# One expert's first weights in transfers of 112, 8 and 8 rows: a mixture-of-experts decoder layer on one core

## The chip, the cores and the metric

The kernel runs on one core of one Trainium2 chip. The metric is the device time of one execution in microseconds (us), as the median of three runs; lower is better. The profile comes from one further execution.

## The reference

One decoder layer over 256 tokens with 1024 features, in float32. Sixteen learned meta tokens are put ahead of the sequence and dropped at the end. With `DEPTH = 1` only the pooling mixer is used, never attention:

```
h = layer_norm(alpha * h + pool_mixer(h))     # trailing means over 2, 4, 8, 16 positions, per-group 256 x 256 matmul
h = layer_norm(alpha * h + moe(h))            # top 4 of 32 experts
```

In `moe` a router picks four of 32 experts for each token. Each expert computes `(clamped_swiglu(x @ w1[e] + b1[e]) @ w2[e] + b2[e]) * gate`, with `w1[e]` of 1024 x 2048 and `w2[e]` of 1024 x 1024 float32 values, 8 MB and 4 MB. All 32 experts have tokens, so some 400 MB of weights are read once from HBM.

## The kernel before

A prologue loads the input, mixes and normalizes it, computes the router's choice, and gives every token a slot in each of its experts. An expert has 64 slots in the main pass; a guarded second pass (`overflow`) covers experts with more tokens.

Then a loop, unrolled in Python, goes over the 32 experts, `for e in range(E)` at line 570. In each step:

- `load_w1` (line 345) issues the loads of `w1[e]`: two tiles of `[128, 4, 2048]`, named `w1t`, one for each half of the contraction. The host has laid out the weights so that partition p of a tile is 32 KB without a gap in HBM. A tile of the first 31 experts is one DMA of 128 rows of 32 KB, 4 MB; for the last expert the second tile comes in three pieces.
- `load_w2` (line 355) issues the loads of `w2`, one expert behind, as one tile `w2t` of the same size. The last expert's `w2` comes in five pieces, `w2h`.
- `mlp_in` (line 388, matmuls at L394) multiplies the gathered tokens by `w1`: 64 matmuls for an expert, 32 on each tile.
- `swiglu` adds the bias, transposes and applies the activation (ACT and DVE); `mlp_out` (matmuls at L443) multiplies by `w2`; `combine` (L462) sums the weighted outputs back into the tokens; `prepare` gathers the tokens of the next two experts (L138).

All weight tiles share one pool of four buffers (`W_BUFS = 4`, tag `"w"`). All their DMAs are issued in program order by SP on one queue. A DMA is issued when PE has read the last of the tile that held the buffer four tiles earlier. One load, `b2r` (33 rows of 4 KB), is issued by ACT on another queue. SP issues nothing but DMAs.

Of the kernel before, what the change touches and what calls it, by code (L numbers as in the profile page):

```python
# [17 lines left out]
P = 128  # L18
# [7 lines left out]
E = 32  # L26
# [8 lines left out]
WARM = 4  # L35
REST = 8
LEN = N_META + SEQ
AUX = 5 * KC + E + KC * E


@with_exitstack
def moe_trunk(ctx: ExitStack, tc: tile.TileContext, x, pool_w, aux_in, b1_in, w1, w2, w2_last, b2, out):
    nc = tc.nc
# [15 lines left out]
    def bank_t(i=None):  # L59
        if i is None:  # L60
            i = turns[0] = 1 - turns[0]
        return bank(f"t{i}", 1)
# [4 lines left out]
    def bank_o(i=None):  # L67
        if i is None:
            i = turns[1] = (turns[1] + 1) % 3
        return bank(f"o{i}", 1)  # L70
# [18 lines left out]
    b2r = const.tile([E + 1, D], F32, name="b2r")  # L89
    aux = const.tile([P, AUX], F32, name="aux")  # L90
    b1 = const.tile([P, 2 * KC * E], F32, name="b1")
# [63 lines left out]
    with tc.tile_pool(name="pro", bufs=1) as pro:  # L155

        xT = pro.tile([P, KC, LEN], F32, name="xT")
        zT = xT[:, :, N_META:]  # L160
# [48 lines left out]
        def pool(g):  # L209
# [3 lines left out]
            while 2 * n < wd:  # L213
                s2 = pro.tile([P, 2, LEN], F32, tag=f"s{n % 3}", name="s2")
                nc.vector.tensor_tensor(s2[:, :, 2 * n - 1:], s[:, :, 2 * n - 1:], s[:, :, n - 1:LEN - n], op=ALU.add)
                s, n = s2, 2 * n
            o, lo = uT[:, g], N_META
            if wd == 2:
                nc.vector.tensor_tensor(o, v[:, :, lo - 1:LEN - 1], v[:, :, lo:], op=ALU.subtract)
            else:  # L220
                nc.vector.tensor_tensor(o, s[:, :, lo:], s[:, :, lo - n:LEN - n], op=ALU.add)
                nc.vector.scalar_tensor_tensor(o, v[:, :, lo:], -float(wd), o, op0=ALU.mult, op1=ALU.add)
# [71 lines left out]
        def last_row(row, dst):  # L294
            for i in range(2):
                nc.scalar.copy(dst[:, i * 512:(i + 1) * 512], spread(row, i, bank_y()))
# [45 lines left out]
    acc = work.tile([P, NT, D], F32, name="acc")  # L342


    def load_w1(src, pieces=((0, 4), (0, 4))):
        v = src.rearrange("(i p j) f -> i p j f", p=P, j=4)
        ts = []
        for i, js in enumerate(pieces):
            wt = wpool.tile([P, 4, 2 * D], F32, tag="w", name="w1t")
            for j, j2 in zip(js, js[1:]):  # L350
                nc.sync.dma_start(out=wt[:, j:j2], in_=v[i][:, j:j2])
            ts.append(wt)
        return lambda k: ts[k // 4][:, k % 4, :]

    def load_w2(src, js=(0, KC)):
        v = src.rearrange("(p j) f -> p j f", j=KC)
        wt = wpool.tile([P, KC, D], F32, tag="w", name="w2t")
        for j, j2 in zip(js, js[1:]):
            nc.sync.dma_start(out=wt[:, j:j2], in_=v[:, j:j2])
        return lambda k: wt[:, k, :].rearrange("p (c o s) -> p o c s", c=2, o=2)  # L360
# [14 lines left out]
    def slot_rows(d, gate, to=bank_t):  # L375

        dg = work.tile([P, NT, 2, CAP], F32, tag="dg", name="dg", bufs=1)
        nc.vector.tensor_mul(dg, d, gate.unsqueeze(3).to_broadcast([P, NT, 2, CAP]))
        s = work.tile([P, 2, SEQ], F32, tag="srow", name="srow", bufs=2)
        p = to()  # L380
        for t in range(NT):
            nc.tensor.transpose(p[:, t * P:(t + 1) * P], dg[:, t].rearrange("p i s -> p (i s)"), ident)
        nc.scalar.copy(s[:, 0], p[:, :SEQ])
        nc.scalar.copy(s[:CAP, 1], p[CAP:, :SEQ])
        nc.scalar.copy(s[CAP:, 1], p[:CAP, :SEQ])
        return s

    def mlp_in(xcols, w1k):
        ph = [bank_h() for _ in range(2)]
        for k in range(KC):  # L390
            wk = w1k(k)
            for u in range(2):
                for hf in range(2):
                    last[k // 4] = nc.tensor.matmul(ph[u][hf * CAP:(hf + 1) * CAP], lhsT=xcols(k),  # L394
                                                    rhs=wk[:, u * D + hf * 512:u * D + (hf + 1) * 512],
                                                    start=(k == 0), stop=(k == KC - 1))
        return ph
# [57 lines left out]
    def outputs():  # L455
        return work.tile([P, 2, 512], F32, tag="y", name="y", bufs=2)

    def combine(y, s, first=False):
        for t in range(NT):
            for o in range(2):  # L460
                p = bank_o()
                nc.tensor.matmul(p, lhsT=s[:, o, t * P:(t + 1) * P], rhs=y[:, o, :], start=True, stop=True)  # L462
                a = acc[:, t, :].rearrange("p (c o s) -> p o c s", c=2, o=2)[:, o]
                pv = p.rearrange("p (c s) -> p c s", c=2)
                if first:
                    nc.vector.tensor_copy(a, pv)
                else:
                    nc.vector.tensor_add(a, a, pv)  # L468
# [70 lines left out]
    def prepare(pair, to=bank_t, banks=(bank_o, bank_o)):  # L539
        d = dispatched(place[:, :, 2 * pair:2 * pair + 2])  # L540
        s = slot_rows(d, gates[:, :, 2 * pair:2 * pair + 2], to)
        xg = columns()
        gather(d, xg, banks)
        pairs[pair] = s, outputs(), xg

    def finish(e, to=bank_y):
        pair, i = divmod(e, 2)
        mlp_out(acts[e], w2s[e], pairs[pair][1], i, to)
# [9 lines left out]
    def by_tile(v):  # L558
        return v.rearrange("p (c o s) -> p o c s", c=2, o=2)

    def onto(y, s, cols, i=None, last=False):

        for t in range(NT):
            for o in range(2):
                r, v = (slice(0, P), o) if i is None else (rows_of(o, 0), o ^ i)
                w = nc.tensor.matmul(z[t][o][:, cols], lhsT=s[r, v, t * P:(t + 1) * P], rhs=y[r, o, cols],  # L566
                                     start=False, stop=last, skip_group_check=True)
        return w

    for e in range(E):  # L570
        pair, i = divmod(e, 2)
        w1k = load_w1(w1[e], ((0, 4), (0, 4) if e < E - 1 else (0, 2, 3, 4)))

        for x in range(max(e - 1, 0), e + (e == E - 3)):
            if e <= E - 3:
                w2s[x] = load_w2(w2[x])
        if i == 0:
            xg = pairs[pair][-1]
        ph = mlp_in(lambda k: xg[k // 4][:, k % 4, i * CAP:(i + 1) * CAP], w1k)
        if e == 0:  # L580
            with tc.issue_after(last[1].ins):
                pairs[0] = slot_rows(d0, gates[:, :, 0:2]), outputs(), xg0
        elif e < E - 3 and i and pair:
            s, y, _ = pairs[pair - 1]
            with tc.issue_after(last[0].ins):
                combine(y, s, pair == 1)
        elif e == E - 3:
            s, y, _ = pairs[pair - 1]
            with tc.issue_after(last[0].ins):
                onto(y, s, slice(0, 512))  # L590
        if e == E - 4:
            z += [[bank_o(), bank_o()], [bank_o(), bank_t(1)]]
            for t in range(NT):
                for o in range(2):
                    nc.tensor.matmul(z[t][o], lhsT=ident, rhs=by_tile(acc[:, t])[:, o], start=True, stop=False,
                                     skip_group_check=True)
        if 0 < e < E - 4:
            finish(e - 1)
        acts[e] = swiglu(ph, b1T[:, :, e, :], (bank_t, bank_t) if e < E - 4 else (t0, bank_y))
        if E - 4 <= e < E - 2:  # L600
            finish(e - 1)
        if e == E - 1:

            nc.scalar.activation(root, acts[e][:, 0, 0:1], AF.Sqrt, scale=0.0, bias=eps_out)
        if i and e < E - 3:
            prepare(pair + 1)
        if e == REST:
            with tc.issue_after(last[1].ins):
                add_rest()
        if e == REST + 4:  # L610
            with tc.issue_after(last[1].ins):
                last_row(b1nT, b1_b)
        if e == E - 3:
            prepare(pair + 1, t0, (bank_h, bank_h))
            finish(e, t0)
            s, y, _ = pairs[pair]
            onto(y, s, slice(0, 512))
# [81 lines left out]
```

## Time and profile before

| what | value |
|---|---|
| median of 3 runs | 969.16 us (969.06 to 969.58) |
| the profiled execution, its own time | 969.38 us |
| its span in the profile | 967.5 us |
| PE busy | 888.6 us, 92% |
| bytes moved by DMA | 407.09 MB, mean 421 GB/s |
| DMA transfers of `w1t` | 66, of which 63 of 4096 KB |

The span is the time from the first to the last instruction in the trace; some 1.9 us of the execution's time lie around it. PE is the matmul engine, DVE and ACT the vector and the scalar engine; SP is the engine that issues the DMAs, and its rows in the timelines are those issues. "DMA share" is the mean busy share of the core's 16 DMA engines.

### The profile page before, as it was taken

The page shows a single profiled execution, that of the slowest core. Times are in us where ns is not written, and L with a number is a line of the kernel's source. Part 1 is how long each engine was busy: PE and PEld are TensorE (multiplying, and loading weights), DVE is VectorE, ACT ScalarE, POOL GpSimd, SP SyncE. Part 2 cuts the span into 40 slices and gives each one's busy share as a digit, 9 for nine tenths or more (in the row PEclk, how much of TensorE's full clock was granted, in tenths as well). Part 3 has the DMA queues.
Part 4 walks back from the last instruction along what each step waited for, and adds up shares of the span by engine and source line. Part 5 has one row for each costly group of instructions (what it writes and reads, how often), then busy time and mean ns, then how long its engine had stood idle before and what let it go on. Part 6 is the DMA issues. An engine that isn't in the chain of part 4 may idle for free.

```text
span 967.5 us, 9682 instructions
## 1 busy us (share of the span) xinstructions
PE 888.6 (92%) x4229; PEld 374.3 (39%) x4229; DVE 237.8 (25%) x495; ACT 132.8 (14%) x271; POOL 1.1 (0%) x9
## 2 busy tenths in 40 slices
PE   9999898989899998998988989799898989999995
PEld 7443333424334343443433434343333433334332
DVE  7331122212043131121311223122121311212024
ACT  1320110201002010020201102011010100102011
POOL 0000000000000000000000000000000000000000
PEclk9999999999999999999999999999999999999998
DMA  9999999999999999999999999999999999999992
GB/s 380 429 430 431 434 430 430 433 427 429 431 430 431 429 431 428 433 429 430 433 429 428 430 430 429 433 432 433 431 429 431 428 428 429 433 433 428 429 415 112
DMA packets 16649, 407.09 MB, mean 421 GB/s; under 512 B 1851, under 2 KB 1979, under 8 KB 3420
## 3 DMA queue, kind: packets, MB, share of 16 engines
q1 hardware_dynamic: 16560, 406.30, 98.0%
q8 instruction: 35, 0.57, 0.2%
q10 hardware_dynamic: 44, 0.14, 0.1%
q14 instruction: 10, 0.08, 0.0%
HBM read 405.38 MB, written 1.05 MB: 420 GB/s over the span
## 4 chain that ended last, share of the span: by engine, by line
PE 53%; DMA 44%; DVE 1%; issue 0%; ACT 0%; DVEq 0%; ACTq 0%
DMA w1t<-in_w 39%; PE ps_h L394 25%; PE ps_y L443 11%; PE ps_o L138 5%; PE ps_o L462 5%; DMA w2t<-in_w 3%; DMA w2h<-in_w_last 2%; PE ps_t L406 2%; PE ps_t L180 1%; PE ps_t L443 1%; PE ps_o L566 1%; PE ps_y L103 0%; PE ps_o L489 0%; PE ps_y L451 0%; PE ps_h L227 0%; PE ps_h L138 0%
## 5 line engine op out<-in xcount | busy, mean ns | idle before, releaser
L394 PE MATMUL ps_h<-w1t,xg 128*64 128x512 f32 x2048 | 469.7, 613 | 48.7 <-DMA w1t<-in_w 48.6
L394 PEld LDWEIGHTS ps_h<-w1t,xg 128*64 128x64 f32 x2048 | 157.5, 141 | 345.0 <-issue 336.7
L443 PE MATMUL ps_y<-w2t,act 128*64 128x512 f32 x928 | 205.5, 595 | 9.9 <-DMA w2t<-in_w 9.1
L408 DVE TENSOR_TENSOR a<-ps_t,b 128x512 f32<-128x512 f32 x60 | 41.5, 692 | 403.4 <-PE ps_t L406 400.3
L443 PEld LDWEIGHTS ps_y<-w2t,act 128*64 128x64 f32 x928 | 67.6, 137 | 128.4 <-issue 113.6
L403 ACT COPY hs<-ps_h 128x512 f32<-128x512 f32 x64 | 37.5, 585 | 351.7 <-PE ps_h L394 351.7
L468 DVE TENSOR_TENSOR acc<-acc,ps_o 128x512 f32<-128x512 f32 x48 | 33.0, 687 | 134.8 <-PE ps_o L462 134.8
L138 PE MATMUL ps_o<-disp,h 128*128 128x128 f32 x448 | 59.1, 275 | 0.0
L138 PEld LDWEIGHTS ps_o<-disp,h 128*128 128x128 f32 x448 | 55.4, 192 | 7.0 <-issue 7.0
L434 DVE COPY y<-ps_y 64x512 f32<-64x512 f32 (+1 forms) x30 | 20.4, 679 | 121.5 <-PE ps_y L443 120.6
L462 PE MATMUL ps_o<-y,srow 128*128 128x512 f32 x104 | 48.1, 605 | 0.0
L432 ACT COPY y<-ps_y 64x512 f32<-64x512 f32 (+1 forms) x30 | 17.2, 572 | 208.7 <-DVE y L434 208.7
L143 ACT ACTIVATE xg<-ps_o,aux 128x128 f32<-128x128 f32 x56 | 21.1, 455 | 177.2 <-PE ps_o L138 177.2
L406 PE MATMUL ps_t<-ident,hs 128*128 128x128 f32 x240 | 39.3, 286 | 1.9 <-ACT hs L403 0.5
L406 PEld LDWEIGHTS ps_t<-ident,hs 128*128 128x128 f32 x240 | 25.2, 141 | 32.0 <-ACT hs L403 30.1
L462 PEld LDWEIGHTS ps_o<-y,srow 128*128 128x128 f32 x104 | 18.7, 189 | 29.2 <-issue 29.2
L416 DVE TENSOR_TENSOR a<-a,sig 128x512 f32<-128x512 f32 x32 | 22.1, 692 | 11.2 <-ACT sig L414 11.1
L414 ACT ACTIVATE sig<-a 128x512 f32<-128x512 f32 x32 | 20.1, 630 | 30.5 <-DVE a L412 28.0
L146 DVE TENSOR_SCALAR xg<-ps_o,aux 128x128 f32<-128x128 f32 x60 | 22.8, 404 | 2.8 <-PE ps_o L138 2.7
L418 DVE SCALAR_TENSOR_TENSOR act<-a,a 128x512 f32<-128x512 f32 x32 | 22.0, 687 | 0.6
L415 DVE TENSOR_SCALAR a<-a 128x512 f32<-128x512 f32 x32 | 13.4, 420 | 0.0
L412 DVE TENSOR_SCALAR a<-a 128x512 f32<-128x512 f32 x32 | 13.3, 417 | 0.0
(163 smaller groups left out, 253.0 us busy)
## 6 DMA issues: line engine op xcount, KB each, us to landing
w1t<-in_w SPq DMA_DIRECT2D x63, 4096.0 KB, 30.2
w2t<-in_w SPq DMA_DIRECT2D x30, 4096.0 KB, 29.0
w2t<-in_w SPq DMA_DIRECT2D x4, 1024.0 KB, 26.8
w2h<-in_w_last SPq DMA_DIRECT2D x3, 1024.0 KB, 19.9
w1t<-in_w SPq DMA_DIRECT2D x1, 2048.0 KB, 26.6
w1t<-in_w SPq DMA_DIRECT2D x2, 1024.0 KB, 29.7
xT<-in_x SPq DMA_DIRECT2D x2, 544.0 KB, 5.3
pw<-in_pool_w SPq DMA_DIRECT2D x2, 512.0 KB, 6.4
```

Source lines behind the costliest of these rows:

```text
L138: nc.tensor.matmul(p[:, (k % n) * P:(k % n + 1) * P], lhsT=h[:, t, k * P:(k + 1) * P], rhs=d[:, t].rearrange("p i s -> p (i s)"), start=(t ...
L143: gx = nc.scalar.activation(xg[0][:, k, :], pk, AF.Identity, scale=g0T[:, k:k + 1], bias=b0T[:, k:k + 1])
L146: nc.vector.tensor_scalar(xg[1][:, k - 4, :], pk, g0T[:, k:k + 1], b0T[:, k:k + 1], op0=ALU.mult, op1=ALU.add)
L394: last[k // 4] = nc.tensor.matmul(ph[u][hf * CAP:(hf + 1) * CAP], lhsT=xcols(k), rhs=wk[:, u * D + hf * 512:u * D + (hf + 1) * 512], start ...
L403: nc.scalar.copy(hs, ph[u])
L406: nc.tensor.transpose(pt[:, j * P:(j + 1) * P], hs[:, j * P:(j + 1) * P], ident)
L408: nc.vector.tensor_add(a, pt.rearrange("p (c s) -> p c s", s=CAP), bias[:, :, u].unsqueeze(2).to_broadcast([P, KC, CAP]))
L416: nc.vector.tensor_mul(gate, gate, sig)
L418: nc.vector.scalar_tensor_tensor(act.rearrange("p c s -> p (c s)"), up.rearrange("p c s -> p (c s)"), 1.0, gate.rearrange("p c s -> p (c s ...
L443: nc.tensor.matmul(py[o], lhsT=act[:, 2 * j + hf, :], rhs=wk[:, o], start=(n == 0), stop=(n == KC - 1))
L462: nc.tensor.matmul(p, lhsT=s[:, o, t * P:(t + 1) * P], rhs=y[:, o, :], start=True, stop=True)
L468: nc.vector.tensor_add(a, a, pv)
```

## The change

`load_w1` gets a list of row ranges, and issues one DMA for each range in place of one for all 128 rows. The list has the one range 0 to 128 for all experts but the 17th (`e == 16`); there it is 0 to 112, 112 to 120 and 120 to 128. The 17th expert's `w1` is thus moved by six DMAs, for each of its two tiles 112 rows (3584 KB), eight rows (256 KB) and eight rows (256 KB). Bytes, buffers, order and everything else stay.

```
+APART = ((0, P - 16), (P - 16, P - 8), (P - 8, P))
...
-    def load_w1(src, pieces=((0, 4), (0, 4))):
+    def load_w1(src, pieces=((0, 4), (0, 4)), rows=((0, P),)):
...
             for j, j2 in zip(js, js[1:]):
-                nc.sync.dma_start(out=wt[:, j:j2], in_=v[i][:, j:j2])
+                for r, r2 in rows:
+                    nc.sync.dma_start(out=wt[r:r2, j:j2], in_=v[i][r:r2, j:j2])
...
-        w1k = load_w1(w1[e], ((0, 4), (0, 4) if e < E - 1 else (0, 2, 3, 4)))
+        w1k = load_w1(w1[e], ((0, 4), (0, 4) if e < E - 1 else (0, 2, 3, 4)),
+                      APART if e == E // 2 else ((0, P),))
```

## Rows read from the trace of the kernel before

**Rows 1.** The page: span, busy time by engine, the chain that ended last.

```profile
span 967.5 us, 9682 instructions
...
PE 888.6 (92%) x4229; PEld 374.3 (39%) x4229; DVE 237.8 (25%) x495; ACT 132.8 (14%) x271; POOL 1.1 (0%) x9
...
PE 53%; DMA 44%; DVE 1%; issue 0%; ACT 0%; DVEq 0%; ACTq 0%
```

**Rows 2.** The page's DMA part: all packets, then queue, kind, packets, MB, share.

```profile
DMA packets 16649, 407.09 MB, mean 421 GB/s; under 512 B 1851, under 2 KB 1979, under 8 KB 3420
...
q1 hardware_dynamic: 16560, 406.30, 98.0%
q8 instruction: 35, 0.57, 0.2%
q10 hardware_dynamic: 44, 0.14, 0.1%
```

**Rows 3.** Windows of 100 us in mid-run; last columns PE clock, DMA share, GB/s.

```profile
400.00:500.00 100.00, 91.95 (x438) 38.28 (x433) 21.71 (x43) 12.90 (x28) 0.00 (x0) 0.98 1.00 430
500.00:600.00 100.00, 92.66 (x436) 39.14 (x436) 25.18 (x49) 13.50 (x28) 0.00 (x0) 0.97 1.00 430
```

**Rows 4.** Waits of the engines: who waited for whom, us, times, longest.

```profile
PE ps_h L394 <- DMA w1t<-in_w: 48.6, 26, 3.1
...
PE ps_y L443 <- DMA w2t<-in_w: 9.1, 8, 1.3
```

**Rows 5.** Waits of SP's queue before it issues, in the same columns.

```profile
SPq L359 <- PE ps_h L394: 285.9, 30, 18.6
SPq L351 <- PE ps_y L443: 242.8, 28, 11.9
SPq L351 <- PE ps_h L394: 227.0, 30, 11.3
```

**Rows 6.** The chain of waits from 895 us to the end: start, us, what.

```profile
899.33 26.61 DMA w1t<-in_w
925.96 19.91 DMA w2h<-in_w_last
945.92 1.95 PE ps_h L451 x16
```

**Rows 7.** DMA issues: count, KB of each, median us from issue to landing.

```profile
w1t<-in_w SPq DMA_DIRECT2D x63, 4096.0 KB, 30.2
w2t<-in_w SPq DMA_DIRECT2D x30, 4096.0 KB, 29.0
...
w1t<-in_w SPq DMA_DIRECT2D x1, 2048.0 KB, 26.6
w1t<-in_w SPq DMA_DIRECT2D x2, 1024.0 KB, 29.7
...
aux<-in_aux SPq DMA_DIRECT2D x1, 164.0 KB, 3.1
b2r<-in_b ACTq DMA_DIRECT2D x1, 132.0 KB
```

**Rows 8.** Line 351 from 400 to 600 us: ns of an issue, and landing times.

```profile
L351 SPq DMA_DIRECT2D w1t<-in_w x13: 327/328/328, 401.3 to 578.0; - x13
...
DMA to landing us min/median/max: 26.7/30.3/32.4
```

**Rows 9.** SP's timeline around the 17th expert's two loads: start, us, what.

```profile
448.77 10.08 SPq L351 DMA_DIRECT2D w1t<-in_w  x2
471.41 0.33 SPq L359 DMA_DIRECT2D w2t<-in_w  x1
```

**Rows 10.** PE's timeline at the 17th expert's two halves of L394.

```profile
481.25 7.09 PE L394 MATMUL ps_h<-w1t,xg 128*64 128x512 f32 x32
491.06 8.78 PE L394 MATMUL ps_h<-w1t,xg 128*64 128x512 f32 x32 [2.72 <-DMA w1t<-in_w]
```

## The prediction, made before the change was run

> **What bounds the kernel now.** I read the page from the top, then views by time. First the busy shares and the chain that ended last [rows 1]: PE is busy 92% of the span, which looks like a PE-bound kernel, but the chain is 44% DMA, nearly all of it `w1t`, and the two take turns. Second the DMA part [rows 2]: the main queue's packets fill 98.0% of sixteen engines' time. Third the windows [rows 3]: in mid-run the DMA share is 1.00 and 430 GB/s are moved in both stretches, while PE has 7 to 8 us to spare in each 100. So the sixteen DMA engines never rest, and PE waits for them: the waits [rows 4] put 48.6 us before L394 to `w1t`, in 26 waits of at most 3.1 us. The reader is to see that a microsecond more work for the slowest DMA engine is a microsecond more kernel, while a microsecond of SP's time costs nothing: SP itself waits hundreds of microseconds for PE to free a buffer [rows 5].
>
> The end says the same. The last steps of the chain [rows 6] are 26.61 us of a `w1t` transfer, at once followed by 19.91 us of a `w2h` transfer, and only from 945.92 us on PE and DVE set the pace. What delays the transfers therefore delays the end one for one.
>
> **What a transfer is made of.** The issues [rows 7] show 63 + 1 + 2 of `w1t`; a whole tile is 4096 KB, 128 rows of 32 KB. The main queue's issues, twelve groups on SP from the first row to `aux`, add up to 115, and its 16560 packets [rows 2] are 115 x 144, so each 128-row transfer is 128 row packets and 16 closing ones: sixteen engines, eight rows each. The small queue q10 carried `b2r`, 33 rows of 4 KB, in 44 packets: 33 and 11, so eleven engines with three rows each. Engines are thus counted by what divides the rows. At 430 GB/s an engine moves 26.9 GB/s, and a 32 KB row takes 1.22 us; a tile is 8 x 1.22 = 9.75 us.
>
> **The change, part by part.** Two tile transfers become six. (a) The two of 112 rows: sixteen engines with seven rows each, 8.53 us instead of 9.75, so -1.22 us on every engine and tile. (b) The four of eight rows: eight rows can occupy at most eight engines, one row each. Those eight get two more rows a tile; the other eight get nothing. (c) Four more issues on SP at 0.328 us [rows 8], 1.3 us. They are covered: the two issues for the 17th expert lie at 448.77 us and ten later, and SP next issues at 471.41 [rows 9], after waiting for PE. A transfer lands 26.7 to 32.4 us after its issue, some three transfers deep. Without that cover they would cost 1.3 us. (d) 32 more closing packets (2 x 16 + 4 x 8 against 2 x 16); under (b)'s bounds they vanish. Nothing moves on PE, ACT or DVE.
>
> So the sum hangs on the price of an eight-row transfer to the eight engines that carry it. Lower bound: each engine moves its row at its own speed, 1.22 us. Upper bound: rate goes with the number of partitions written, 8/128 of 430 GB/s, and the 262 KB take 9.75 us, eight times as long. Large transfers that write few neighbouring partitions do not occur in this trace; each big one spreads over all 128, where every engine might well have a way into SBUF to itself. The nearest row is q10, the one load of less than 128 rows. Its 0.1% (0.05 to 0.15%) of 16 x 967.5 = 15,480 us are 7.7 to 23 us for 0.14 MB, 55 to 166 us per MB; q1 has 15,170 us for 406.30 MB, 37.3 us per MB. So 33 rows cost 1.5 to 4.4 times as much per byte. Their packets are short, and that may be a part of it: q8, 16 KB packets, has 23 to 39 us for 0.57 MB, 1.1 to 1.8 times. I take four times, inside the q10 bounds and towards their upper end, because eight neighbouring rows are fewer than 33: 4.87 us for each eight-row transfer.
>
> The sum for those eight engines: 7 + 4 + 4 = 15 row times a tile in place of 8, 7 x 1.22 = 8.5 us, and 17.1 us for two tiles. I count all four on the same eight engines; if they took turns on all sixteen, half of it would be left. Against the profiled execution's own 969.38 us (a span of 967.5 and 1.9 around it) that is 986.5; the median of the runs is 0.2 lower, 986.
>
> [...]
>
> **What is late next.** PE starts the 17th expert's two halves at 481.25 and 491.06, the second after 2.72 us of waiting [rows 10]. It would start them some 8 and 17 us later; nothing gives this back, since DMA is full in every later window [rows 3]. The other eight engines run ahead into the queued transfers and then idle.
>
> **The rivals.**
> *The rows share nothing, and the eight engines were ahead.* Instruction packets (q8, 0.2%) take 23 to 39 us of engine time. If these fall on the eight engines that the short transfers spare, those end the run 2.9 to 4.8 us behind, about 3.9. Taking two rows (2.43 us) from them and giving two to the others moves the last arrival from 3.9 to max(3.9 - 2.43, 2.43) = 2.43 us: 1.5 us gained, 967.7. For it: instruction packets exist and must fall somewhere. Against it: no view names their engines. It ends on the other side, faster by over 0.2% (1.9 us, about what a measurement of this kernel can tell from no change), only when the halves differ by 4.4 us or more: then up to 2.4 us gained, 966.8. I give this rival 0.28: 0.22 within 0.2%, 0.06 faster.
> *The rows share nothing, and the eight engines were not ahead.* Then two rows more are on the slowest engine: +2.43 us, 971.6, slower by 0.25%. For it: DMA busy at 1.00 throughout leaves no engine slack to absorb it. Chance 0.10.
> *The change is hidden.* DMA would need slack later; the windows show none. It is inside the first rival's 0.22.
>
> **How the numbers follow.** The forecast, eight-row transfers well above one row time, has 0.62. Its own range: at twice a row time 7 + 2 + 2 = 11 rows a tile, +7.3 us, 976.5; at the 4.4 of q10's upper bound 15.8 rows, +19 us, 988.2; I put 976 to 990. At eight times it would be +36.6 us, 1006, which I leave out above, with about 0.1. Since the no-change cases hold over 0.2, the whole range reaches down to 967.5, which leaves out only the best of the first rival. Slower 0.62 + 0.10 = 0.72, same 0.22, faster 0.06.
>
> **What the profile of the changed kernel would show.** q1 should have 16560 + 32 = 16592 packets; another number says that the rows were split over other engines. The issue list should show `w1t` x2 of 3584 KB and x4 of 256 KB, and x61 whole. If the forecast holds, mean GB/s falls to about 413 (407.09 MB in 985 us), the waits of L394 for `w1t` rise from 48.6 us by about 17, two of them by some 8 us each between 480 and 520 us, the 256 KB transfers land late, and all from there to the end is shifted by one amount. If the waits near 480 us rise by 2 us or less, the rows share nothing, and a shift at the end of 1 to 2 us in either direction tells the two rivals apart. The prediction is wrong if eight engines write eight neighbouring rows at full speed; then its largest term, 17.1 us, is gone.

## The result

| | before | after |
|---|---|---|
| median of 4 runs | 969.2 us (969.06 to 969.58) | 999.4 us (997.94 to 1000.17) |
| ratio | | 1.0309, 95% interval 1.0291 to 1.0327 |
| the profiled execution, its own time and its span | 969.38, 967.5 | 999.78, 998.0 |

The change costs 30.2 us, 3.1%. The prediction had the direction, but 986 us, and a range that ends at 990. Lines of the body stand three lower than before: L394 is L397, L351 is L354.

The page of the changed kernel, the lines that answer to [rows 1] and [rows 2], with the granted clock and the GB/s in 40 slices:

```profile
span 998.0 us, 9691 instructions
...
PE 888.2 (89%) x4229; PEld 373.5 (37%) x4229; DVE 238.0 (24%) x495; ACT 132.9 (13%) x271; POOL 1.1 (0%) x9
...
PEclk9999999999999999999779999999999999999998
DMA  9999999999999999999999999999999999999992
GB/s 382 434 426 435 427 433 430 430 431 429 430 431 430 432 429 431 429 431 369 198 247 429 433 431 429 430 431 430 431 428 433 429 430 430 429 433 428 427 409 79
DMA packets 16681, 407.09 MB, mean 408 GB/s; under 512 B 1883, under 2 KB 2011, under 8 KB 3452
...
q1 hardware_dynamic: 16592, 406.30, 97.8%
```

PE's work is the same to 0.4 us. Nearly all of the loss lies in three slices near the middle, where GB/s fall from 430 to 198. The DMA line says 9 there as everywhere: the engines were busy, and slow. The packets are the 16592 that were forecast, which fits the counts of engines assumed there. The same stretch in windows of 10 us (in the kernel before these seven windows have 423 to 442 GB/s):

```profile
460.00:470.00 10.00, 10.00 (x53) 5.03 (x53) 2.17 (x4) 1.51 (x4) 0.00 (x0) 1.00 1.08 364
470.00:480.00 10.00, 9.72 (x56) 4.71 (x54) 5.36 (x13) 2.91 (x6) 0.00 (x0) 1.00 0.98 216
480.00:490.00 10.00, 1.30 (x8) 0.14 (x2) 0.68 (x1) 0.58 (x1) 0.00 (x0) 0.71 1.03 175
490.00:500.00 10.00, 3.01 (x8) 1.00 (x10) 0.00 (x0) 0.00 (x0) 0.00 (x0) 0.50 0.98 211
500.00:510.00 10.00, 6.22 (x26) 1.66 (x22) 0.00 (x0) 0.00 (x0) 0.00 (x0) 0.93 1.07 226
510.00:520.00 10.00, 0.00 (x0) 0.00 (x0) 0.00 (x0) 0.00 (x0) 0.00 (x0) 0.58 0.91 210
520.00:530.00 10.00, 8.72 (x32) 2.92 (x32) 0.00 (x0) 0.51 (x1) 0.00 (x0) 0.74 0.98 419
```

The last two columns say it: the DMA share stays near 1, the rate is half. Against 430 GB/s the seven windows lack 66 + 214 + 255 + 219 + 204 + 220 + 11 = 1189 GB/s for 10 us each, which at 430 GB/s is 27.7 us, nearly the whole loss. The half rate already holds from 470 to 480 us, where the first 112-row transfer must run, and not only at the eight-row ones; that is the first sign of which step failed.

The issues, the waits of PE, PE's timeline at the 17th expert's two halves and the next expert's first, and two steps of the chain of waits, in answer to [rows 7], [rows 4], [rows 10] and [rows 6]:

```profile
w1t<-in_w SPq DMA_DIRECT2D x61, 4096.0 KB, 30.1
...
w1t<-in_w SPq DMA_DIRECT2D x2, 3584.0 KB, 50.7
...
w1t<-in_w SPq DMA_DIRECT2D x4, 256.0 KB
```

```profile
PE ps_h L397 <- DMA w1t<-in_w: 79.3, 27, 15.7
```

```profile
496.99 9.23 PE L397 MATMUL ps_h<-w1t,xg 128*64 128x512 f32 x32 [15.69 <-DMA w1t<-in_w]
...
521.27 9.03 PE L397 MATMUL ps_h<-w1t,xg 128*64 128x512 f32 x32 [15.05 <-DMA w1t<-in_w]
...
542.05 8.78 PE L397 MATMUL ps_h<-w1t,xg 128*64 128x512 f32 x32 [3.34 <-DMA w1t<-in_w]
```

```profile
930.14 26.62 DMA w1t<-in_w
956.77 19.87 DMA w2h<-in_w_last
```

The two 3584 KB transfers take 50.7 us from issue to landing in the median, where a whole tile takes 30.1. PE waits 15.69 and 15.05 us for the two halves, and the last two steps of the chain stand 30.8 us later than in [rows 6], with the same lengths: one shift, never given back. From 490 to 500 us the granted clock of PE is 0.50 of full, and the first half's 32 matmuls, begun at 496.99, take 9.23 us in place of the 7.09 of [rows 10]; since PE then waits 15.05 us for the second half anyway, that adds nothing.

### The profile page after: what moved, and what is told of

Its sections match the earlier page's. It is cut to its first block, busy times and chain, and to the rows that moved or that the text cites. A ratio compares the mean times of both kernels' runs of the same rounds, so it can differ in the third digit from the quotient of the medians.

```text
span 998.0 us, 9691 instructions
## 1 busy us (share of the span) xinstructions
PE 888.2 (89%) x4229; PEld 373.5 (37%) x4229; DVE 238.0 (24%) x495; ACT 132.9 (13%) x271; POOL 1.1 (0%) x9
## 3 DMA queue, kind: packets, MB, share of 16 engines
q1 hardware_dynamic: 16592, 406.30, 97.8%
## 4 chain that ended last, share of the span: by engine, by line
PE 53%; DMA 43%; another core or an unknown queue 2%; DVE 1%; ACT 0%; issue 0%; SPq 0%; DVEq 0%; ACTq 0%
DMA w1t<-in_w 36%; PE ps_h L397 25%; PE ps_y L446 11%; DMA w2t<-in_w 5%; PE ps_o L140 4%; PE ps_o L465 4%; DMA w2h<-in_w_last 2%; PE ps_t L409 1%; PE ps_t L182 1%; PE ps_t L446 1%; PE ps_o L569 1%; PE ps_y L105 0%; PE ps_o L492 0%; PE ps_y L454 0%; PE ps_h L229 0%
## 5 line engine op out<-in xcount | busy, mean ns | idle before, releaser
L397 PE MATMUL ps_h<-w1t,xg 128*64 128x512 f32 x2048 | 469.2, 612 | 79.4 <-DMA w1t<-in_w 79.3
L397 PEld LDWEIGHTS ps_h<-w1t,xg 128*64 128x64 f32 x2048 | 157.0, 141 | 376.4 <-issue 350.5
L409 PEld LDWEIGHTS ps_t<-ident,hs 128*128 128x128 f32 x240 | 25.2, 140 | 32.0 <-ACT hs L406 30.1
## 6 DMA issues: line engine op xcount, KB each, us to landing
w1t<-in_w SPq DMA_DIRECT2D x61, 4096.0 KB, 30.1
w1t<-in_w SPq DMA_DIRECT2D x2, 3584.0 KB, 50.7
```

The lines of the kernel that those rows point to most:

```text
L409: nc.tensor.transpose(pt[:, j * P:(j + 1) * P], hs[:, j * P:(j + 1) * P], ident)
```

## The experiments

All edit the loads of the 17th expert's first weights alone, unless said otherwise. Times are medians, "+" is against the kernel before, run beside it on the same chip (969.2 to 969.5 us). The theories, as the expectations name them: A, engines that write partitions which share a way into SBUF (a path that several partitions would have in common; no view shows one) slow each other (in the forecast this was the price of the eight-row transfers alone); B, more and shorter transfers cost something each; C, balance, the two extra rows on eight of the engines; D, the slowness is on the reading side, in HBM.

**More transfers, all rows (e1).** The two tiles are cut by columns into three DMAs each.

```
-        w1k = load_w1(w1[e], ((0, 4), (0, 4) if e < E - 1 else (0, 2, 3, 4)))
+        w1k = load_w1(w1[e], ((0, 2, 3, 4), (0, 2, 3, 4)) if e == E // 2 else
+                      ((0, 4), (0, 4) if e < E - 1 else (0, 2, 3, 4)))
```

> The 17th expert's two tiles are moved in three transfers each, as in the change, but cut by columns: all 128 rows, with 16, 8 and 8 KB of each row. Theory A (shared ways: packets slow one another when engines write partitions that share a way into SBUF, and a 128-row transfer avoids that): no slowing, 969 to 970 us. Theory B (price of more and shorter transfers): about what the change cost, 999 us. Theory C (balance: the cost is the two extra rows on eight engines): 969 us.

969.4 us, ratio 1.0002 (0.9993 to 1.0012). Six transfers in place of two cost 0.2 us, within the interval; B falls.

**Fewer, balanced pieces (e2, e3), and one tile alone (e4).**

```
-APART = ((0, P - 16), (P - 16, P - 8), (P - 8, P))
+APART = ((0, P - 16), (P - 16, P))           # e2
+APART = ((0, P // 2), (P // 2, P))           # e3
-                for r, r2 in rows:
+                for r, r2 in (rows if i == 0 else ((0, P),)):   # e4
```

> 112 and 16 rows for each of the two tiles: every engine has eight rows again, and no transfer has eight. Theory A: the 112-row packets stay at about 2.4 us in place of 1.22, 7 x 1.2 x 2 = +17 us, and the 16 rows cost some 3 us more a tile: 985 to 997 us. Theory B: half as many transfers added, +15, 984 us. Theory C: balanced, 969 us.

> 64 and 64 rows for each of the two tiles, four rows on every engine each time. Theory A: sixteen engines write half of the partitions; if these hold half of the ways, every packet takes twice 1.22 us and a tile 19.5 us in place of 9.75: +19.5 us, 988 to 989 us. Theory B: +15, 984 us. Theory C: balanced, 969 us.

> The change on the first of the 17th expert's two tiles alone. If each tile pays for itself (A, B and C alike): half of 30, 984 us. If the two disturb each other, as a queue that has come apart would: less than half, 975 to 980 us.

e2: 996.0 us, ratio 1.0277 (1.0259 to 1.0294), +26.8. e3: 993.1, 1.0243 (1.0226 to 1.0261), +23.9. e4: 986.9, 1.018 (1.0163 to 1.0197), +17.7. In e2 and e3 every engine has, if rows are counted as in the prediction (7 + 1 and 4 + 4), eight rows a tile, as before, and most of the loss stays: C falls, and with it the picture of the sum, in which only the engines of the short transfers pay. e4 costs a little more than half of the whole.

**Which side of the transfer (e5 to e8).** The first tile alone as sixteen transfers of eight rows: neighbours on both sides (e5), four apart on both sides (e6), four apart in SBUF alone (e7), four apart in HBM alone (e8).

```
+NEAR = [slice(8 * m, 8 * m + 8) for m in range(16)]
+SPREAD = [slice(32 * b + c, 32 * b + c + 29, 4) for b in range(4) for c in range(4)]
+EIGHTS = tuple(zip(NEAR, NEAR))    # SBUF, HBM; e6 SPREAD, SPREAD; e7 SPREAD, NEAR; e8 NEAR, SPREAD
...
-                nc.sync.dma_start(out=wt[:, j:j2], in_=v[i][:, j:j2])
+                for a, b in (rows if i == 0 else WHOLE):
+                    nc.sync.dma_start(out=wt[a, j:j2], in_=v[i][b, j:j2])
```

> The first tile of the 17th expert goes in sixteen transfers of eight neighbouring rows, the second whole. Eight engines have 16 rows in place of eight. Theory C (balance alone): 8 x 1.22 = +9.8 us, 979 us. Theory A: eight neighbouring partitions share two ways, packets of 3.3 us (as seen near 485 us in the changed kernel) to 4.9 us, 16 of them in place of eight at 1.22: +43 to +68 us, 1012 to 1037 us.

> The same sixteen transfers of eight rows, but the eight rows of each are four apart (c, c+4, ... c+28 of a block of 32), in SBUF and in HBM. Same number, size and engines as with neighbouring rows. Theory A, with a way for every four neighbouring partitions: eight ways for eight engines, packets of about 1.22 us, +10 us, 979 us. Theory B and a theory that any eight-row transfer is slow: as with neighbouring rows, 1012 us or more.

> Sixteen transfers of eight rows that are four apart in SBUF but neighbours in HBM; the rows of the tile's weights are thereby in another order, so the 17th expert computes with rows in the wrong place. Theory A (the way into SBUF): about 979 us. Theory D (the reading side: eight neighbouring rows of HBM are slow): as with neighbouring rows, 1012 us or more.

> Sixteen transfers of eight rows that are neighbours in SBUF but four apart in HBM; the 17th expert again computes with rows in the wrong place. Theory A: as with neighbouring rows, 1012 us or more. Theory D: about 979 us.

| | SBUF | HBM | us | ratio | |
|---|---|---|---|---|---|
| e5 | neighbours | neighbours | 999.8 | 1.0326 (1.0305 to 1.0348) | +30.6 |
| e8 | neighbours | four apart | 995.7 | 1.027 (1.0253 to 1.0287) | +26.5 |
| e6 | four apart | four apart | 985.2 | 1.0166 (1.0149 to 1.0183) | +16.0 |
| e7 | four apart | neighbours | 984.9 | 1.0163 (1.0146 to 1.018) | +15.7 |

What decides is which partitions are written together: e7 is e6, and e8 is near e5. D falls as the main cause; that e8 is 4 us below e5, clear of the intervals, is not explained by any run. The window from 470 to 480 us, first of e5, then of e6, and e6's next one:

```profile
470.00:480.00 10.00, 10.00 (x58) 4.74 (x56) 5.37 (x13) 2.91 (x6) 0.00 (x0) 1.00 0.55 139
```

```profile
470.00:480.00 10.00, 10.00 (x58) 4.75 (x56) 5.36 (x13) 2.91 (x6) 0.00 (x0) 1.00 0.50 211
480.00:490.00 10.00, 2.68 (x14) 0.66 (x10) 0.68 (x1) 0.58 (x1) 0.00 (x0) 0.83 0.93 223
```

From 470 to 480 us the DMA share in e6 is 0.50, and 211 GB/s are moved, half of 430: what eight engines would move, each at the rate it has in a whole tile. In e5, with eight neighbours, a little more of the engines' time (0.55) moves 139. The sizes missed: e6 and e7 came out 6 us above their expectation, e5 and e8 below theirs. One thing behind them lies with SP, whose seventeen issues for the 17th expert last until 481.62 us in e6 (the two of [rows 9] end at 458.85):

```profile
448.67 32.95 SPq L356 DMA_DIRECT2D w1t<-in_w  x17
```

Between 440 and 500 us SP waited 26.1 us for `w1t` transfers to land before it issued more. The second tile is the last of the seventeen, so it starts late, and from 470 to 480 us half of the engines' time goes unused (share 0.50). The totals of e5 to e8 hold this cost as well, and are not the price of partitions alone; their comparison, sixteen transfers of one size each, stands.

**The 112-row transfer with an easier rest, and other splits of all 128 rows (e9 to e12).**

```
+APART = [slice(0, P - 16)] + [slice(P - 16 + c, P - 3 + c, 4) for c in range(4)]   # e9
+APART = [slice(c, P - 1 + c, 2) for c in range(2)]                                 # e10
+APART = [slice(c, P - 3 + c, 4) for c in range(4)]                                 # e11
+APART = [slice(32 * c, 32 * c + 32) for c in range(4)]                             # e12
...
-                nc.sync.dma_start(out=wt[:, j:j2], in_=v[i][:, j:j2])
+                for r in rows:
+                    nc.sync.dma_start(out=wt[r, j:j2], in_=v[i][r, j:j2])
```

> Both tiles of the 17th expert: rows 0 to 111 as one transfer, as in the change, and then the last sixteen rows as four transfers of four rows each, four apart (112, 116, 120, 124, and so on). Each of these short transfers writes four different groups of four partitions. If the 112-row transfers themselves run at half speed (packets of about 2.4 us in place of 1.22, seven rows a tile and engine: 2 x 7 x 1.2 = 16.5 us), and only the rest of the change's +30 us is due to the eight neighbouring rows, about +16 to +24, 985 to 993. If the 112-row transfers are slowed only because the short ones of eight neighbouring rows run beside them, the loss goes with those: at four engines with four rows more at 1.22 us, +5 to +10, 974 to 979.

> Both tiles as the even rows and then the odd rows, 64 each, so both transfers write all groups of four neighbouring partitions; against the 64 neighbouring rows of the earlier run (+23.9 us). If what costs is that the rows of a transfer lie in few groups of partitions: well under it, 969 to 980. If what costs is that two engines write one group of four at the same time, which sixteen engines with four rows each do here as there (an engine with rows eight partitions long covers two groups, and two engines' rows fall into each pair of groups): +16 to +24, 985 to 993. If only a transfer of the whole 128 rows is fast, 985 or above as well.

> Both tiles as four transfers of 32 rows four apart: every group of four partitions is written once in each transfer. Two rows per engine and transfer. If the spread over groups decides, under +8, 969 to 977. If engines that share a group of partitions at one time decide (the sixteen engines hold two groups each here, each its own, so nothing is shared within a transfer, but packets of two successive transfers can meet): 969 to 985, and less than the even and odd rows. If only whole transfers are fast, 990 or above.

> Both tiles as four transfers of 32 neighbouring rows: each reaches eight groups of four partitions, with sixteen engines. If the groups of partitions decide: slower than 64 neighbouring rows (+23.9 us), +25 to +45, 994 to 1014. If the loss is the same whenever a transfer is not whole (half speed for two tiles): +20 to +25, 989 to 994.

| | pieces of a tile | us | ratio | |
|---|---|---|---|---|
| e9 | 112, then 4 x 4 rows four apart | 1001.0 | 1.0328 (1.0311 to 1.0345) | +31.5 |
| e10 | even rows, odd rows | 969.4 | 0.9997 (0.9987 to 1.0006) | -0.1 |
| e11 | 4 x 32 rows four apart | 969.6 | 1.0001 (0.9992 to 1.0011) | 0.0 |
| e12 | 4 x 32 neighbours | 993.2 | 1.0245 (1.0227 to 1.0262) | +23.7 |

The window from 480 to 490 us, first of e10, then of e12:

```profile
480.00:490.00 10.00, 8.31 (x38) 2.79 (x34) 0.68 (x1) 0.58 (x1) 0.00 (x0) 1.00 1.00 430
```

```profile
480.00:490.00 10.00, 2.45 (x12) 0.57 (x8) 0.68 (x1) 0.58 (x1) 0.00 (x0) 0.76 1.00 211
```

The same bytes in more transfers: 430 GB/s or 211, by the choice of partitions alone. So it is not that only a whole tile is fast. Nor is it the number of neighbours in a row: 32 neighbours cost what 64 do (+23.7, +23.9), where the theory of groups of partitions had them cost more. And e9, whose short pieces are spread, costs no less than the change (+31.5, +30.2): the 112-row transfers themselves must be slow, which no theory about the short ones explains (e16 below tests it without any short ones).

**Which partitions slow each other (e13 to e15).** By then three theories stood, none of them read from a view: A1, a way serves four neighbouring partitions and the four that lie 32 further; A2, a way serves eight neighbours; F, an engine is fast only on the partitions that it carries in a whole tile. e13 puts 120 and 8 rows into the kernel; e14 and e15 leave the kernel as it was and add single transfers, and groups of three, behind its end (the rows of a transfer in brackets). e14 and e15 are one execution each.

```
+APART = ((0, 120), (120, P))                                     # e13
+    nc.sync.dma_start(out=wp[0:112], in_=vp[0:112])              # e14, 27 such pairs
+    nc.vector.tensor_copy(probe[:, 1:2], wp[:, 0, 0:1])
+    nc.sync.dma_start(out=wa[0:112], in_=vp[0:112])              # e15, 14 groups; wb and wc likewise,
+    nc.vector.tensor_copy(probe[:, 0, 1:2], wa[:, 0, 0:1])       # then the three copies
```

> Both tiles of the 17th expert as rows 0 to 119 and then 120 to 127. 120 rows are fifteen engines with eight rows each. If eight neighbouring partitions are a way of their own and the engine's rows are neighbours, the 120 rows run at full speed (only 112, in sevens, straddle), and only the eight rows at the end cost: +5 to +9 us, 974 to 979. If four neighbours and the four that lie 32 further share a way, engines carry neighbours and so meet in pairs: half speed again, +22 to +32, 991 to 1002. If an engine is fast only on the partitions that it carries in a whole tile: the same +22 to +32.

> The kernel before, and behind its end 27 single transfers of 32 KB rows into one tile, each waiting for the one before, with nothing beside them. Time from issue to landing, less what a single row takes above 1.22 us. Theory A1 (a way serves four neighbouring partitions and the four that lie 32 further; two engines on a way get half each; rows dealt out in blocks of neighbours): 128 rows 9.7; rows 0 to 63 9.7, 32 to 95 4.9; 64 rows two apart 4.9 to 9.7; 0 to 31 4.9; 16 neighbours, 8 neighbours and 4 neighbours all 4.9; 8 rows four apart 1.2 from row 0 and from row 64 alike; 2 rows 32 apart 2.4, 64 apart 1.2; 112 rows 10.9, 120 rows 19.5, 96 rows 12.2. Theory A2 (a way serves eight neighbours): 8 neighbours 9.7, 8 rows four apart 2.4, 16 rows eight apart 1.2, 32 to 95 9.7. Theory F (an engine is fast only on the partitions that it carries in a whole tile): 8 rows four apart 1.2 from row 0 and 2.4 from row 64; 112 rows 17.

> The kernel before, and behind its end 14 groups of three transfers into three tiles, the three issued one right after the other, the groups waiting for each other. Landing of the last of three, less the fixed part of a single transfer. If engines on a way settle apart when transfers follow each other (A1 with time to settle): three of 112 rows some 26 to 33 us, three of 0 to 63 29 us, three of eight neighbours 14.6 us, 112 to 119 and 120 to 127 by turns less than that. If an engine stays at half speed wherever its partitions are not those of a whole tile (F): three of 112 rows 51 us. Three whole tiles 29 us by all.

e13: 1001.4 us, ratio 1.0334 (1.0317 to 1.0352), +31.9: the +22 to +32 expected by A1 and F, not the +5 to +9 by A2. SP's timeline of e14 behind the kernel's end. Each issue waits until the transfer before has landed, so from one issue to the next is one transfer and a fixed part:

```profile
965.75 0.34 SPq L666 DMA_DIRECT2D wp<-in_w  x1
978.14 0.35 SPq L668 DMA_DIRECT2D wp<-in_w  x1
995.41 0.31 SPq L670 DMA_DIRECT2D wp<-in_w  x1
1012.75 0.39 SPq L672 DMA_DIRECT2D wp<-in_w  x1
1035.28 0.32 SPq L674 DMA_DIRECT2D wp<-in_w  x1
1052.21 0.57 SPq L676 DMA_DIRECT2D wp<-in_w  x1
1065.20 0.58 SPq L678 DMA_DIRECT2D wp<-in_w  x1
1072.94 0.52 SPq L680 DMA_DIRECT2D wp<-in_w  x1
1080.99 0.32 SPq L682 DMA_DIRECT2D wp<-in_w  x1
1088.44 0.48 SPq L684 DMA_DIRECT2D wp<-in_w  x1
1093.82 0.32 SPq L686 DMA_DIRECT2D wp<-in_w  x1
...
1128.90 0.28 SPq L698 DMA_DIRECT2D wp<-in_w  x1
1135.41 0.73 SPq L700 DMA_DIRECT2D wp<-in_w  x1
1139.53 0.65 SPq L702 DMA_DIRECT2D wp<-in_w  x1
1143.57 0.58 SPq L704 DMA_DIRECT2D wp<-in_w  x1
...
1168.77 0.49 SPq L714 DMA_DIRECT2D wp<-in_w  x1
1173.59 0.47 SPq L716 DMA_DIRECT2D wp<-in_w  x1
1177.52 0.23 SPq L718 DMA_DIRECT2D wp<-in_w  x1
```

The fixed part is about 2.7 us: the whole tile of L666 has an interval of 12.39, of which 9.75 are its eight rows on each engine, and L716, two rows on two engines 64 partitions apart, takes 3.93, of which one row is 1.22. Engines are counted by what divides the rows, and the packets bear that out: q1 has 17833 in e14, 1273 more than before, and the 27 transfers have 969 rows and by this count 304 closing packets. The other intervals, less 2.7:

| line, rows of the transfer | interval | less 2.7 | each engine at 1.22 us a row | by A1 |
|---|---|---|---|---|
| L668, 0 to 111 | 17.27 | 14.6 | 8.5 | 10.9 |
| L670, 16 to 127 | 17.34 | 14.6 | 8.5 | 10.9 |
| L672, 0 to 119 | 22.53 | 19.8 | 9.75 | 19.5 |
| L674, 0 to 95 | 16.93 | 14.2 | 7.3 | 12.2 |
| L676, 0 to 63 | 12.99 | 10.3 | 4.9 | 9.7 |
| L678, 32 to 95 | 7.74 | 5.0 | 4.9 | 4.9 |
| L680, 64 rows two apart | 8.05 | 5.4 | 4.9 | 4.9 to 9.7 |
| L682, 0 to 31 | 7.45 | 4.8 | 2.4 | 4.9 |
| L698, 112 to 119 | 6.51 | 3.8 | 1.2 | 4.9 |
| L700, 8 rows four apart from 0 | 4.12 | 1.4 | 1.2 | 1.2 |
| L702, 8 rows four apart from 64 | 4.04 | 1.3 | 1.2 | 1.2 |
| L714, 2 rows 32 apart | 4.82 | 2.1 | 1.2 | 2.4 |

A2 falls by L678 (5.0 us, not 9.7) and L700 (1.4, not 2.4), F by L702: eight rows four apart take 1.3 us from row 64, as from row 0 (1.4), where F has 2.4. Of the three A1 alone is left: what it has slow is slow in this table, and what it has fast is fast. Rows 0 to 63 take twice as long as rows 32 to 95 (10.3 and 5.0 us), which are as many bytes on as many engines; two rows 32 apart slow each other (L714, 4.82 us from issue to issue), and 64 apart hardly (L716, 3.93). Eight neighbours were a little cheaper than the four turns of 1.22 us that A1 gives them: 3.8 us for 112 to 119, not 4.9. And 112 and 96 rows took 14.6 and 14.2 us, longer than equal shares on each way give (10.9, 12.2). So A1 says that they are slowed, and not by how much.

The column "by A1" needs one thing more, the order in which rows are dealt to the engines, which no view shows. Blocks of neighbours, which it takes, fit the transfers of rows 0 to 119 (19.8 us against 19.5), 0 to 63 (10.3, 9.7) and 0 to 31 (4.8, 4.9). They do not fit those that run over all 128 partitions. There, by A1 with blocks, each engine would share its ways with the one whose rows lie 32 further, from the first row to the last, and by an estimate from 1.22 us a row the whole tile (L666) would take 19.5 us, 64 rows two apart (L680) 9.8, and 32 rows four apart (L684) 4.9. They took 9.7, 5.4 and, with an interval of 5.38, 2.7 us. So A1 with blocks does not hold for these, whether by the order of the rows or by A1 itself, and it is the last two that were free in e10 and e11 (-0.1 and 0.0 us). Why 128 rows take 9.7 us and 120 take 19.8 is not shown.

In e15 the copies of DVE mark the landings; the last of three whole tiles, three 112-row transfers, the first of 120 rows, and at the end a group of 112, 8 and 8 rows as in the change:

```profile
997.26 0.15 DVE L671 COPY probe<-wc 128x1 f32<-128x1 f32 x1 [9.92 <-DMA wc<-in_w]
1012.24 0.15 DVE L675 COPY probe<-wa 128x1 f32<-128x1 f32 x1 [14.82 <-DMA wa<-in_w]
1027.02 0.15 DVE L676 COPY probe<-wb 128x1 f32<-128x1 f32 x1 [14.63 <-DMA wb<-in_w]
1041.06 0.15 DVE L677 COPY probe<-wc 128x1 f32<-128x1 f32 x1 [13.88 <-DMA wc<-in_w]
1061.07 0.15 DVE L681 COPY probe<-wa 128x1 f32<-128x1 f32 x1 [19.86 <-DMA wa<-in_w]
...
1252.74 0.15 DVE L741 COPY probe<-wa 128x1 f32<-128x1 f32 x1 [13.88 <-DMA wa<-in_w]
1256.87 0.15 DVE L742 COPY probe<-wb 128x1 f32<-128x1 f32 x1 [3.98 <-DMA wb<-in_w]
1261.35 0.15 DVE L743 COPY probe<-wc 128x1 f32<-128x1 f32 x1 [4.32 <-DMA wc<-in_w]
```

One 112-row transfer lands every 14 to 15 us, with a whole tile or its like ahead of it. That is between the two expectations (26 to 33 us for three by A1, 51 by F; from 997.26 to 1041.06 it is 43.8): the third transfer takes hardly less than the first (14.0 against 15.0 us from landing to landing), so no settling apart shows.

**The two terms by themselves in the stream (e16, e17), and half a tile (e18).** Of each tile only rows 0 to 111 (e16), only the two eight-row transfers (e17, here rows 0 to 7 and 8 to 15), or only rows 0 to 63 (e18) are moved and multiplied.

```
+APART = ((0, P - 16),)               # e16, n = 112
+APART = ((0, 8), (8, 16))            # e17, n = 16
+APART = ((0, P // 2),)               # e18, n = 64
...
-        ph = mlp_in(lambda k: xg[k // 4][:, k % 4, i * CAP:(i + 1) * CAP], w1k)
+        n = 112 if e == E // 2 else P
+        ph = mlp_in(lambda k: xg[k // 4][:n, k % 4, i * CAP:(i + 1) * CAP], w1k)
```

> The changed kernel without the four eight-row transfers: of the 17th expert's first weights only rows 0 to 111 of each tile are moved, and its first matmuls sum over 112 rows of each tile (the last sixteen are left out). If a 112-row transfer costs in the stream what its windows show (3.67 MB at 215 GB/s, 17.1 us against 9.75 for the whole tile): 2 x 7.3 = +14.7 us, 984. If it costs there what it costs alone (14.6 us): +9.7, 979. If it runs at full speed beside nothing small, as the prediction had it (8.53 us): -2.4, 967.

> The changed kernel without the two 112-row transfers: of each of the 17th expert's two first tiles only two transfers of eight neighbouring rows, 0 to 7 and 8 to 15, are moved, and its first matmuls sum over these sixteen rows (the rest is left out). By the prediction's 4.87 us each: four take 19.5 us on their engines, as long as two whole tiles: no change, 969. By what they took one after another behind 112 rows (4.1 to 4.5 us): 16.5 to 18 against 19.5, -1.5 to -3, 966 to 968. If those engines are slowed further by the other eight, that are then ahead by two tiles: above 970.

> As the first of these with rows 0 to 63 alone (the other 64 of each tile are left out). By bytes half of a tile: -9.7 us, 959. By the ways that 64 neighbours reach (9.7 to 10.3 us for the half as for a whole tile): no change, 969 to 970, and up to +4 with what follows it.

e16: 986.4 us, ratio 1.0173 (1.0156 to 1.019), +17.1. e17: 964.8, 0.9945 (0.9929 to 0.9962), -4.5. e18: 974.8, 1.0053 (1.0036 to 1.007), +5.5. e16 and e18 came out above everything that was expected of them, e17 below. The window from 470 to 480 us of e16, in which nothing small is anywhere in the queue:

```profile
470.00:480.00 10.00, 10.00 (x58) 4.84 (x56) 5.36 (x13) 2.91 (x6) 0.00 (x0) 1.00 1.00 223
```

Two whole tiles are 2 x 9.75 = 19.5 us of every engine. So a 112-row transfer is worth (19.5 + 17.1) / 2 = 18.3 us in the stream, more than the 14.6 it takes alone, and an eight-row one (19.5 - 4.5) / 4 = 3.75 us, or a little less: GB/s fall to 412 and 414 in two later windows of e17 (500 to 520 and 540 to 560 us, PE busy throughout), some 0.8 us each that the eights need not answer for. Moving half of the 17th expert's first weights, rows 0 to 63 (e18), takes longer than moving all of them. PE's clock, at 0.50 of full from 490 to 510 us in e18, is not the reason: GB/s stand at 429 from 500 us on, and the 15.3 us that the four windows from 460 to 500 us lack against 430 GB/s (357, 210, 198, 299), less 9.75 us for the bytes left out, are the 5.5.

## Why the prediction was right in direction and wrong in size

- **What bounds the kernel.** Right. The lost DMA time came out at the end nearly one for one: the seven windows lack 27.7 us, the chain's last transfers begin 30.8 us later [rows 6], and PE's busy time is unchanged. The other 3 us are not located.
- **Step (a), the two 112-row transfers at "8.53 us instead of 9.75, so -1.22 us on every engine and tile".** This is the step that failed. They were taken at full speed, with no upper bound, since "each big one spreads over all 128" was read as if 112 were as good. Measured by e16: 18.3 us in place of 8.53, so 19.5 us were missing from the sum for two. With 8.53 us for the large ones and the measured price of the eights the sum would give +12.6 us, inside the stated range. That sixteen engines with seven rows each meet on the ways is what A1 says of them, and no view shows it; it fits in kind, and not in size (10.9 us by A1, 14.6 alone in e14). The trace of before had no transfer like it, just as it had none of eight rows, and that was the reason that gave step (b) bounds.
- **Step (b), 4.87 us for each eight-row transfer.** Right in kind: above one row time, below eight. It is 3.8 us alone (e14), 4.1 and 4.5 from landing to landing behind a 112-row transfer (e15), and 3.75 in the stream (e17), three times a row. Four of them are 4.5 us cheaper than in the sum. That all of them lie on the same eight engines, as the sum has it, fits the share of 0.50 in e6, while sixteen such transfers follow each other.
- **The sum.** With the measured terms 2 x 18.3 + 4 x 3.75 - 19.5 = +32.1 us, against +30.2 measured; the terms of separate runs add up to within 2 us. The forecast's +17.1 had the eights carrying all of it and the 112 rows gaining. In fact e16, without any eight-row transfer, loses 17.1; that the two figures agree is chance.
- **The picture that eight engines pay, while "the other eight engines run ahead into the queued transfers and then idle".** Wrong for the 112 rows, where the share of all sixteen is 0.98 at 216 GB/s; e2, with every engine at eight rows, loses 26.8 us.
- **Steps (c) and (d), issues and closing packets.** Right: e1 has as many transfers, and no fewer packets, for 0.2 us, within its interval.
- **The rivals.** Two of them had the rows share nothing; e10 against e12 (969.4 and 993.2 us) settles that the time depends on which rows go together, and a gain by balance could not show. The third needed slack in later windows: the slices of the page show 430 GB/s again from the 22nd on, and nothing is given back.
- **Signs.** Right in kind: 16592 packets, the three kinds of issue, mean GB/s down (408; 413 forecast), two late halves, one shift to the end. The halves were late by 15.7 and 30.2 us (481.25 to 496.99, 491.06 to 521.27 [rows 10]) in place of 8 and 17. The profile gives no landing time for the 256 KB transfers.
- **What stays open.** Why 112 rows take 14.6 us alone when equal shares give 10.9, and 18.3 in the stream. That engines which are out of step cross each other's ways, with the whole tiles behind included, would do it; that was argued, not shown. e6 points that way: its spread rows by themselves move 211 GB/s at a share of 0.50, whole tiles 430 at 1.00, and from 480 to 490 us, with both in the queue, 223 GB/s are moved at a share of 0.93. How rows are dealt to the engines is open as well: blocks of neighbours were taken from three fits, do not fit the three transfers over all 128 partitions (L666, L680, L684), and no view names engines.

## What to carry to other kernels

The price of a DMA into SBUF depended here on which partitions it writes together (e5 +30.6 us, e7 +15.7), so a load cut by rows must be priced for every piece, the large one too: here 112 of 128 rows were twice as slow as all 128 (18.3 against 9.75 us), while cuts by columns (e1) or into every second (e10) or fourth row (e11) were free: +0.2, -0.1 and 0.0 us. Where a load like this one must be cut, try columns first, or every second or fourth row over all partitions. That a piece has nearly all rows is not enough: 0 to 119 took 19.8 us alone, all 128 rows 9.7 (e14). And read GB/s beside the DMA share, which stood at 1.00 while half of the rate was lost (e12, 211 GB/s). A quantity without a row in the trace gets bounds on both sides, also when it looks like a small change of one that has a row.

## What the runs showed of the hardware that was not expected

- Half a tile, rows 0 to 63, is no cheaper than a whole one: alone it took 10.3 us, 128 rows 9.7 (e14), and in the kernel moving this half of the weights cost 5.5 us more than moving all (e18).
- A transfer of 64 rows, 32 to 95, takes half of a whole tile's time (5.0 us, e14), one of rows 0 to 63 does not (10.3 us).
- 120 rows in one transfer (19.8 us) take twice as long as 128 (9.7 us), each alone (e14).
- Eight neighbouring rows needed 3.8 us (112 to 119), where A1 had four rows one after another at 1.22 us, 4.9.
